# Address residues of matmul operands in a hybrid attention layer: unpadded key rows, small tiles in a pool of their own, padded projection weights

## The chip, the cores and the metric

The kernel runs on one core of one Trainium2 chip. A core has five engines that run beside each other: TensorE (PE in the profile, with its weight loads as PEld), VectorE (DVE), ScalarE (ACT), GpSimd (POOL) and SyncE (SP, which here issues most DMAs). The metric is the device time of one execution in microseconds (us), as the median of several runs. The profile is of one execution, with a span of its own.

A matmul takes two operands from the on-chip memory SBUF: a stationary one (128 columns here, brought in by a weight load of its own) and a moving one (up to 512 columns that stream past). The product is summed in PSUM. SBUF is 128 partitions, and a tile occupies the same byte range in each. "Residue" below means the byte at which an operand begins in its partition, modulo 512.

## The reference

One encoder layer on 2048 tokens of width 1024, all in float32. A combined projection feeds two groups of heads.

```python
h = x @ w_in                        # 1024 -> 2528 columns, split into the parts below
# group A: gated linear attention, 4 heads, key width 64, value width 128, chunks,
#          a forward and a backward scan, summed, RMSNorm per head, SiLU gate
o_a = gla_branch(g_q, g_k, g_v, g_gate, ...)
# group B: latent attention, 4 heads; dense softmax over all 2048 keys
q = (rms_norm(c_q) @ w_uq);  kv = (rms_norm(c_kv) @ w_ukv)
s = q_nope @ k_nope.T + q_rope @ k_rope.T
o_b = softmax(s) @ v * silu(gate)
x = layer_norm(alpha * x + concat(o_a, o_b) @ w_out)
```

## The kernel before, in words

**Split products.** Each float32 operand is held as two tiles of type float32r: a high part, rounded by a copy on ScalarE (`hi`, L366), and the rest, a subtraction on VectorE or GpSimd (`lo`, L373). A product is then three matmuls into one PSUM tile: high by high, low by high, high by low. `mm3` (L421, matmuls on L423, L424 and L425) writes them; the scores and two products of sweep C write theirs out by hand.

**Four stages**, in the order of time:

- *Sweep A* (`sweep_a`, L622), 16 chunks of 128 tokens from the last to the first. `products` (L755) multiplies a chunk (stationary: `xah`, `xal`, 8 row blocks k of 128) by the weights `wah` and `wal` (moving), in three column groups of 288, 384 and 384 columns (`A_GROUPS`, L27). The result is `ipa`. For most chunks 24 matmuls of 512 columns for the gate follow (`gate_products`, L842: result `ipg`, moving `wgh`/`wgl`). Between these stand the small products of the linear attention (L902 to L1043) and transposes by the identity.
- *Sweep C* (`sweep_c`, L1111), chunks in pairs from the first to the last: `pz` (L1221, 256 columns), `ipm` (L1292, 448 columns), norms, rotary tables. It leaves, for each of 16 key tiles of 128 keys, the compressed keys `ckvT_h`, `ckvT_l` (L1358, L1361), the rotary keys `kr` (tile name `krs`, L1364) and the values `vh`, `vl` in SBUF for the rest of the kernel. `vh` and `vl` have rows of 128 elements; the three key tiles have rows of `KW` = 132 elements, of which 128 are used (L549 to L551).
- *Attention* (`attention`, L1518), 16 blocks (4 heads by 4 blocks of 512 queries), each over 8 pairs of key tiles. For a pair, `scores` (L1544) writes 2 x 5 matmuls of 512 columns (L1552 to L1556): stationary a key tile, moving a query tile. Then ScalarE copies the scores out (L1561), VectorE keeps a running maximum (L1574), subtracts the maximum (L1598), ScalarE takes the exponential (L1602) and the high part `ph` (L1604), GpSimd the low part `pl` (L1609), and `pv` (L1632) writes 2 x 3 matmuls of 512 columns: stationary `vh`/`vl`, moving `ph`/`pl`. Per block there are three groups of four transposes by the identity (`mx` L1580, `mb` L1592, `sx` L1661) and three matmuls of 512 columns for `y` (L1698). So a block has 80 + 48 + 3 = 131 matmuls of 512 columns and 12 transposes.
- *Output projection* (`OutProj`): 16 chunks; moving `woh`/`wol`, stationary `oh`/`ol`, results `po`, `pmb`, `px` of 512 columns (the last chunk in part 256), residual, LayerNorm, store.

**Order.** The order on each engine is fixed by hand: tables of places (`PLACE`, `PLACE_LAST`, `PLACE_C` and the like) say at which step an operation of a pair is put, and `in_order` (L385) chains what comes out. The edits below change no entry of these tables.

**Places in SBUF.** Pools are laid one after another. Before the change most tiles begin at residue 448 (queries, values, chunks, gate weights, scores `s`). Others do not:

| operand (role) | residue before | residue after |
|---|---|---|
| queries `qh`, `ql`, `rh`, `rl` (moving, scores) | 448 | 448 |
| `ckvT_h`, `krs` of key tile kt (stationary, scores) | 192 + 16 kt | 448 |
| `ckvT_l` of key tile kt (stationary, scores) | 448 + 16 kt | 448 |
| `vh`, `vl` (stationary, pv) | 448 | 448 |
| `ph`, `pl` (moving, pv); `ofh` (moving, y) | 0 | 448 |
| `wah`, `wal`, row block k (moving, ipa) | 448 + 128 k, and 128 more for columns 288 on | 448 |
| `xah`, `xal` (stationary, ipa, ipg); `wgh`, `wgl` (moving, ipg) | 448 | 448 |
| `woh`, `wol` (moving, output projection) | 192 for k < 4, 448 for k >= 4 | 448 |
| `xch`, `xcl` (moving, pz) and `wzh`, `wzl` (stationary, pz) | 192 and 448 | the same |
| identity (moving, transposes) | 128 | 128 |

Row kt of a key tile lies 132 x 4 = 528 = 512 + 16 bytes after the row before it. A row block of `wah` is 1056 x 4 = 4224 = 8 x 512 + 128 bytes long, and its groups begin at columns 0, 288 and 672 (288 x 4 = 2 x 512 + 128; 672 x 4 = 5 x 512 + 128). `ph`, `pl` and `ofh` stand in pool `bp` (L1526) behind two tiles `mc` of 16 bytes, which take 32 bytes each.

Of the kernel before, what the change touches and what calls it, by code (L numbers as in the profile page):

```python
# [18 lines left out]
P = 128  # L19
S = 2048  # L20
D = 1024
NK = D // P
NCH = S // P
H = 4
NA = 1056
W_PIECES = ((2, 2, 2, 2), (2, 2, 2, 2), (2, 2, 2, 1, 1))
A_GROUPS = ((0, 288), (288, 384), (672, 384))  # L27
QB = 512
NQB = S // QB
NKT = S // P  # L30
KW = P + 4
TAU_INV = 1.0 / 16.0
RMS_EPS = 1e-6
LN_EPS = 1e-5
# [324 lines left out]
class K:  # L359
# [145 lines left out]
    def run(self):  # L505
        tc, nc, ins = self.tc, self.nc, self.ins
        with ExitStack() as top:
            cp = top.enter_context(tc.tile_pool(name="const", bufs=1))
            self.cp = cp
            dp = top.enter_context(tc.tile_pool(name="scr", bufs=1, space=DRAM))  # L510
            self.qd_s = [dp.tile([P, H * P], F32, name=f"qd_s{c}") for c in range(NCH)]
            self.oi_s = [dp.tile([P, H * P], F32, name=f"oi_s{c}") for c in range(NCH)]
            self.su_s = [dp.tile([P, H * P], F32, name=f"su_s{c}") for c in range(NCH)]
            self.u_s = [dp.tile([P, H * P], F32, name=f"u_s{c}") for c in range(NCH)]
            self.qa_s = [[dp.tile([P, H, QB], F32, name=f"q{p}_s{b}") for p in "hl"] for b in range(NQB)]
            self.qr_s = [[dp.tile([H, 64, QB], F32, name=f"r{p}_s{b}") for p in "hl"] for b in range(NQB)]
            self.gm_s = [dp.tile([P, H, QB], F32, name=f"gm_s{b}") for b in range(NQB)]
            self.oa_s = [dp.tile([P, H, P], F32, name=f"oa_s{c}") for c in range(NCH)]
            self.r_s = [dp.tile([1, H, QB], F32, name=f"r_s{b}") for b in range(NQB)]
            self.ob_s = [dp.tile([P, H, QB], F32, name=f"ob_s{b}") for b in range(NQB)]  # L520

            ident = cp.tile([P, P], F32, name="ident")
            self.ident = ident
            self.gkv_c = cp.tile([P, 1], F32, name="gkv_c")
            self.gn_c = cp.tile([P, 1], F32, name="gn_c")
            self.cw = cp.tile([P, NCH, 3, H], F32, name="cw")

            psum = ExitStack()
            pspool = lambda n: psum.enter_context(tc.tile_pool(name=n, bufs=2, space=PSUM, reuse_waits="tile"))
            self.gp, self.ip, self.tr = pspool("gp"), pspool("ip"), pspool("tr")  # L530
            self.xfp = top.enter_context(tc.tile_pool(name="xfp", bufs=2, reuse_waits="tile"))
            edge = top.enter_context(tc.tile_pool(name="edge", bufs=1, side="right"))
            edge.tile([P, 8], F32, name="edge")
            self.keep = top.enter_context(tc.tile_pool(name="keep", bufs=1, side="right", reuse_waits="tile"))
            wgs = ExitStack()
            self.wgp = wgs.enter_context(tc.tile_pool(name="wgp", bufs=2 * NK + 1, side="right", reuse_waits="tile"))
            self.xab = wgs.enter_context(tc.tile_pool(name="xab", bufs=2, side="right"))
            self.wgate = []
            self.wl = None
            self.sweep_a()  # L540
            self.wz = top.enter_context(tc.tile_pool(name="wz", bufs=2 * NK + 1, reuse_waits="tile"))
            bcs = ExitStack()
            self.wm = bcs.enter_context(tc.tile_pool(name="wm", bufs=2 * NK + 1, reuse_waits="tile"))
            self.bc = bcs.enter_context(tc.tile_pool(name="bc", bufs=1, reuse_waits="tile"))
            self.wl = bcs.enter_context(tc.tile_pool(name="wl", bufs=2, reuse_waits="tile"))
            self.late_gates()
            wgs.close()
            rp = top.enter_context(tc.tile_pool(name="res", bufs=1, side="right", reuse_waits="tile"))
            self.ckvT_h = rp.tile([P, NKT, KW], F32R, name="ckvT_h")  # L549
            self.ckvT_l = rp.tile([P, NKT, KW], F32R, name="ckvT_l")  # L550
            self.kr = rp.tile([P, NKT, KW], F32R, name="krs")  # L551
            self.vh = rp.tile([P, NKT, P], F32R, name="vh")
            self.vl = rp.tile([P, NKT, P], F32R, name="vl")
            self.sweep_c()
            bcs.close()
            psum.close()
            self.wof = top.enter_context(tc.tile_pool(name="wof", bufs=PRE_W, side="right", reuse_waits="tile"))
            self.attention()
# [63 lines left out]
    def sweep_a(self):  # L622
        tc, nc, ins, cp = self.tc, self.nc, self.ins, self.cp
        with ExitStack() as ctx:
# [1 line left out]
            xp, ip, tr, gp = self.xab, self.ip, self.tr, self.gp  # L626


            wah, wal = (wp.tile([P, NK, NA], F32R, name=f"wa{p}") for p in "hl")
            mask = wp.tile([P, P], I32, name="mask")  # L630
            rmask = wp.tile([P, H, P], F32, name="rmask")
            wg = wp.tile([98, H, P], F32R, name="wg")
# [17 lines left out]
            with tc.tile_pool(name="sta", bufs=1, reuse_waits="tile") as sta:  # L650
# [2 lines left out]
                wgf = sta.tile([98, H * P + 1], F32, name="wgf")  # L653
                wgh = sta.tile([98, H * P], F32R, name="wgh")
                wdone, worder = [], {}
                for g, (c0, n) in enumerate(A_GROUPS):
                    k = 0
                    for m in W_PIECES[g]:
                        if g == 0 and k in (0, NK // 2):
                            xs = slice(k, k + NK // 2)  # L660
                            nc.sync.dma_start(xf[:, xs], ins["xT"][NCH - 1][:, xs])
                            with self.in_order(worder):
                                self.hi(xcur[0][:, xs, 0], xf[:, xs])
                                self.lo(xcur[1][:, xs, 0], xf[:, xs], xcur[0][:, xs, 0])
                        st = sta.tile([P, m, n], F32, name=f"was{g}_{k}")
                        nc.sync.dma_start(st, ins[f"wA{g}"][:, k:k + m])
                        ks, cs = slice(k, k + m), slice(c0, c0 + n)
                        with self.in_order(worder):
                            for e in [slice(j, j + 1) for j in range(m)] if g == 0 else [slice(0, m)]:
                                kh, kl = wah[:, ks, cs][:, e], wal[:, ks, cs][:, e]  # L670
                                ops = self.hi(kh, st[:, e]), self.lo(kl, st[:, e], kh)
                        k += m
                        wdone.append(ops)
                    if g == 1:
                        nc.sync.dma_start(self.ident, ins["ident"])
# [79 lines left out]
    def products(self, d, g, after=lambda g, k: None):  # L755

        nc, c, i, g1 = self.nc, d["c"], d["i"], d["g1"]
        c0, n = A_GROUPS[g]
        xh, xl = d["x"]
        if i == 0 and g == 2:  # L760
            pt = self.gp.tile([P, 1024], F32, tag="gp", name=f"ipa{c}_{g}")
# [594 lines left out]
        self.lo(s["cqT_l"][:, :, j], d["tm"][:, 0:2], s["cqT_h"][:, :, j])  # L1356

    def c_ckvTh(self, d):  # L1358
        self.hi(self.ckvT_h[:, d["c"], :P], d["tm"][:, 2])

    def c_ckvTl(self, d):  # L1361
        self.lo(self.ckvT_l[:, d["c"], :P], d["tm"][:, 2], self.ckvT_h[:, d["c"], :P])

    def c_krT(self, d):  # L1364
        self.hi(self.kr[:, d["c"], :P], d["tm"][:, 3])


    def c_pqr(self, d):
# [149 lines left out]
    def attention(self):  # L1518
# [4 lines left out]
        with ExitStack() as ctx:  # L1523
            qp = self.wz
            sp = ctx.enter_context(tc.tile_pool(name="sp", bufs=NP + 4, reuse_waits="tile"))
            bp = ctx.enter_context(tc.tile_pool(name="bp", bufs=2, reuse_waits="tile"))  # L1526
            bank = lambda n, bufs=1: ctx.enter_context(tc.tile_pool(name=n, bufs=bufs, space=PSUM, reuse_waits="tile"))
            pM, pO, pX, pA, pS = bank("pM"), bank("pO"), bank("pX"), bank("pA"), bank("pS", 2)
            blocks = [(h, b) for b in range(NQB) for h in range(H)]
# [14 lines left out]
            def scores(i, j):  # L1544


                d = stt[i]
                qh, ql, rh, rl = d["q"]
                ps = d["ps", j] = pS.tile([P, 2, QB], F32, tag="pS", name=f"pS{i}_{j}")
                for e in range(2):  # L1550
                    kh, kl, kr = (t[:, 2 * j + e, :P] for t in (self.ckvT_h, self.ckvT_l, self.kr))
                    mm(ps[:, e], kh, qh, start=True, stop=False)  # L1552
                    mm(ps[:, e], kh, ql, start=False, stop=False)  # L1553
                    mm(ps[:, e], kl, qh, start=False, stop=False)  # L1554
                    mm(ps[:, e], kr, rh, start=False, stop=False)  # L1555
                    mm(ps[:, e], kr, rl, start=False, stop=True)  # L1556
# [24 lines left out]

            def rmax(i):
                d = stt[i]
                d["mc"] = bp.tile([P, 4], F32, tag="mc", name=f"mc{i}")
                V.tensor_reduce(d["mc"], d["x"], AX.X, ALU.max)

            def bmax(i):
# [75 lines left out]
            def rcp(i):  # L1663

                d = stt[i]
                rc = bp.tile([P, 4], F32, tag="rc", name=f"rc{i}")
                V.tensor_reduce(rc, d["x"], AX.X, ALU.add)
                V.reciprocal(rc, rc)
                d["rc"] = rc
# [11 lines left out]

            def rows(i):
                h, b = blocks[i]
                rr = bp.tile([4, P], F32, tag="rm", name=f"rt{i}", bufs=1)
                Ac.activation(rr, stt[i]["rt"], AF.Copy)
                nc.sync.dma_start(self.r_s[b][:, h].rearrange("o (e p) -> (o e) p", p=P), rr)

# [358 lines left out]
```

## Time and profile before

| | |
|---|---|
| median of 3 runs | 1305.8 us (1305.19 to 1305.91) |
| span of the profiled execution | 1302.9 us, 2.9 us less than the median |
| sweep A | to about 355 us |
| sweep C | about 355 to 609 us |
| attention | about 609 to 1113 us |
| output projection | about 1113 to 1303 us |
| TensorE busy | 1285.0 us of the span, 7082 matmuls |
| VectorE, ScalarE, GpSimd busy | 963.4, 816.7, 787.8 us |

How to read it: a span given for a matmul runs from its start to the modelled end of its drain, and the next matmul starts before that end. So the busy time of TensorE tells only that matmuls follow each other without a pause. How fast they follow is read from the distance of two starts, called pitch below. With matmuls of 512 columns that follow each other, the span is the pitch and a constant drain.

### The profile page before, as it was taken

How to read it: one execution, taken by the hardware profiler on the slowest of the kernel's cores; microseconds unless marked ns; L12 is line 12 of the kernel's file. 1: busy time of each engine (PE TensorE's matmuls, PEld its weight loads, DVE VectorE, ACT ScalarE, POOL GpSimd, SP SyncE). 2: the span in 40 equal slices, each digit the busy share in tenths (PEclk: the TensorE clock that was granted, in tenths of full speed). 3: DMA queues.
4: the chain of work that ended last, by engine and by line, in shares of the span. 5: the costliest groups of instructions: out<-in, count | busy, mean ns of one | idle time of the engine just before them, and what ended most of it. 6: DMA issues, size and time to landing. Idle time of an engine off the chain costs nothing.

```text
span 1302.9 us, 19959 instructions
## 1 busy us (share of the span) xinstructions
PE 1285.0 (99%) x7082; PEld 1130.4 (87%) x7082; DVE 963.4 (74%) x1706; ACT 816.7 (63%) x1334; POOL 787.8 (60%) x494
## 2 busy tenths in 40 slices
PE   8999999999999999999999999999999999999997
PEld 7999999999999999999788888888888888888886
DVE  7966665656674555554888888888888889469997
ACT  7765656565676566564778788878888888511110
POOL 0143233332467667661488888889999999944441
PEclk9999999999999999999999999999999999999999
DMA  8222213131566556656301111122123210366652
GB/s 293 66 89 61 87 53 94 51 95 49 171 232 194 187 178 205 206 173 213 87 1 41 41 42 41 41 60 63 58 70 99 51 41 9 122 204 205 215 192 98
DMA packets 105795, 145.81 MB, mean 112 GB/s; under 512 B 16630, under 2 KB 59262, under 8 KB 105696
## 3 DMA queue, kind: packets, MB, share of 16 engines
q1 hardware_dynamic: 97632, 142.41, 34.9%
q0 software_dynamic: 672, 2.10, 0.4%
q8 instruction: 56, 0.92, 0.3%
q10 hardware_dynamic: 7392, 0.03, 0.3%
q14 instruction: 43, 0.35, 0.1%
HBM read 94.14 MB, written 50.36 MB: 111 GB/s over the span
## 4 chain that ended last, share of the span: by engine, by line
PE 90%; POOL 2%; DVE 1%; ACT 1%; DMA 1%; issue 1%; DVEq 0%; POOLq 0%; SPq 0%
PE pz L1221 6%; PE ipm L1292 5%; PE o L423 5%; PE o L425 5%; PE o L424 5%; PE pS L1552 4%; PE pS L1555 4%; PE pS L1554 4%; PE pS L1556 4%; PE pS L1553 4%; PE ipa L423 4%; PE ipa L424 4%; PE ipa L425 4%; PE po L425 2%; PE po L423 2%; PE po L424 2%
## 5 line engine op out<-in xcount | busy, mean ns | idle before, releaser
L375 POOL TENSOR_TENSOR pl<-s,ph 128x1024 fp32r<-128x1024 f32 x128 | 306.8, 2411 | 65.8 <-ACT ph L369 60.6
L1574 DVE TENSOR_TENSOR rm<-pS,rm 128x512 f32<-128x512 f32 x210 | 144.8, 690 | 43.7 <-ACT s L1561 38.4
L1561 ACT ACTIVATE s<-pS 128x1024 f32<-128x1024 f32 x128 | 131.2, 1025 | 67.9 <-PE pS L1556 66.0
L1598 DVE TENSOR_TENSOR s<-s,mb 128x1024 f32<-128x1024 f32 x128 | 151.2, 1213 | 9.1 <-PE mb L1592 9.0
L1050 POOL TENSOR_TENSOR Us<-Us,cw 128x512 f32<-128x512 f32 x16 | 20.0, 1247 | 226.8 <-DVE Us L1048 188.3
L369 ACT ACTIVATE ph<-s 128x1024 fp32r<-128x1024 f32 x128 | 135.0, 1056 | 18.2 <-PE o L425 17.7
L1602 ACT ACTIVATE s<-s 128x1024 f32<-128x1024 f32 x128 | 131.4, 1050 | 12.3 <-DVE s L1598 12.2
L423 PE MATMUL ipa<-wah,xah 128*128 128x384 f32 (+1 forms) x384 | 129.6, 338 | 5.4 <-ACT wah L369 5.3
L424 PE MATMUL ipa<-wal,xah 128*128 128x384 f32 (+1 forms) x384 | 125.5, 327 | 0.0
L425 PE MATMUL ipa<-wah,xal 128*128 128x384 f32 (+1 forms) x384 | 124.9, 325 | 0.0
L1552 PE MATMUL pS<-qh,ckvT_h 128*128 128x512 f32 x256 | 103.8, 405 | 0.8 <-ACT s L1602 0.4
L423 PE MATMUL o<-ph,vh 128*128 128x512 f32 x256 | 102.6, 401 | 0.0
L425 PE MATMUL o<-ph,vl 128*128 128x512 f32 x256 | 101.3, 396 | 0.0
L1555 PE MATMUL pS<-rh,krs 128*128 128x512 f32 x256 | 101.2, 395 | 0.0
L424 PE MATMUL o<-pl,vh 128*128 128x512 f32 x256 | 101.1, 395 | 0.0
L1554 PE MATMUL pS<-qh,ckvT_l 128*128 128x512 f32 x256 | 100.9, 394 | 0.0
L1556 PE MATMUL pS<-rl,krs 128*128 128x512 f32 x256 | 100.7, 393 | 0.0
L1553 PE MATMUL pS<-ql,ckvT_h 128*128 128x512 f32 x256 | 100.6, 393 | 0.0
L1625 DVE TENSOR_TENSOR ap<-ap,s 128x512 f32<-128x512 f32 x120 | 83.1, 693 | 2.7 <-ACT s L1602 0.8
L375 POOL TENSOR_TENSOR ol<-of,oh 128x512 fp32r<-128x512 f32 x32 | 43.0, 1346 | 63.9 <-ACT oh L369 63.9
L423 PEld LDWEIGHTS ipa<-wah,xah 128*128 128x128 f32 x384 | 73.1, 190 | 6.2 <-ACT wah L369 5.3
L424 PEld LDWEIGHTS ipa<-wal,xah 128*128 128x128 f32 x384 | 73.2, 191 | 1.0 <-DVE wal L375 0.6
(325 smaller groups left out, 3841.2 us busy)
## 6 DMA issues: line engine op xcount, KB each, us to landing
xcf<-xT_dram SPq DMA_DIRECT2D x16, 512.0 KB, 5.5
xr<-x_dram SPq DMA_DIRECT2D x16, 512.0 KB, 6.5
out_dram<-rr SPq DMA_DIRECT2D x32, 256.0 KB, 2.2
xaf<-xT_dram SPq DMA_DIRECT2D x14, 512.0 KB, 4.2
oib<-oi_s SPq DMA_DIRECT2D x16, 256.0 KB, 4.6
qdb<-qd_s SPq DMA_DIRECT2D x16, 256.0 KB, 4.6
SU<-su_s SPq DMA_DIRECT2D x16, 256.0 KB, 5.0
ub<-u_s SPq DMA_DIRECT2D x16, 256.0 KB, 4.3
```

The source lines that it names most:

```text
L369: return nc.scalar.activation(dst, src, AF.Copy).ins
L375: return e.tensor_tensor(dst, src, hi.bitcast(F32), ALU.subtract).ins
L423: mm(out, ah, bh, start=start, stop=False)
L424: mm(out, ah, bl, start=False, stop=False)
L425: mm(out, al, bh, start=False, stop=stop)
L1552: mm(ps[:, e], kh, qh, start=True, stop=False)
L1553: mm(ps[:, e], kh, ql, start=False, stop=False)
L1554: mm(ps[:, e], kl, qh, start=False, stop=False)
L1555: mm(ps[:, e], kr, rh, start=False, stop=False)
L1556: mm(ps[:, e], kr, rl, start=False, stop=True)
L1574: V.tensor_tensor(d["rm"], src[:, e], d["rm"], ALU.max)
L1598: V.tensor_tensor(s, s, d["mb"][:, None, :].to_broadcast([P, 2, QB]), ALU.subtract)
```

## The change

Three edits; no instruction is added or taken away, and each engine keeps its order.

- Key rows have 128 elements in place of 132 (`KW` is gone), so each key tile kt begins a whole number of 512 bytes after the last.
- The small tiles of attention, `mc`, `rc` and the row tile of `rows`, go from pool `bp` to a new pool `bs` behind it, so the large tiles of `bp` move 64 bytes down.
- The weights of sweep A get rows of 1152 columns in place of 1056, and the three groups start at columns 0, 384 and 768 (`A_PLACE`) in place of 0, 288 and 672. The same columns are computed.

```diff
+NA_PAD = 1152
 A_GROUPS = ((0, 288), (288, 384), (672, 384))
+A_PLACE = (0, 384, 768)
-KW = P + 4
...
-            self.ckvT_h = rp.tile([P, NKT, KW], F32R, name="ckvT_h")
-            self.ckvT_l = rp.tile([P, NKT, KW], F32R, name="ckvT_l")
-            self.kr = rp.tile([P, NKT, KW], F32R, name="krs")
+            self.ckvT_h = rp.tile([P, NKT, P], F32R, name="ckvT_h")
+            self.ckvT_l = rp.tile([P, NKT, P], F32R, name="ckvT_l")
+            self.kr = rp.tile([P, NKT, P], F32R, name="krs")
...
-            wah, wal = (wp.tile([P, NK, NA], F32R, name=f"wa{p}") for p in "hl")
+            wah, wal = (wp.tile([P, NK, NA_PAD], F32R, name=f"wa{p}") for p in "hl")
...
-                        ks, cs = slice(k, k + m), slice(c0, c0 + n)
+                        ks, cs = slice(k, k + m), slice(A_PLACE[g], A_PLACE[g] + n)
...
-        c0, n = A_GROUPS[g]
+        c0, n = A_PLACE[g], A_GROUPS[g][1]
...
     def c_ckvTh(self, d):
-        self.hi(self.ckvT_h[:, d["c"], :P], d["tm"][:, 2])
+        self.hi(self.ckvT_h[:, d["c"]], d["tm"][:, 2])
...
+            bs = ctx.enter_context(tc.tile_pool(name="bs", bufs=2, reuse_waits="tile"))
...
-                d["mc"] = bp.tile([P, 4], F32, tag="mc", name=f"mc{i}")
+                d["mc"] = bs.tile([P, 4], F32, tag="mc", name=f"mc{i}")
...
-                rc = bp.tile([P, 4], F32, tag="rc", name=f"rc{i}")
+                rc = bs.tile([P, 4], F32, tag="rc", name=f"rc{i}")
...
-                rr = bp.tile([4, P], F32, tag="rm", name=f"rt{i}", bufs=1)
+                rr = bs.tile([4, P], F32, tag="rm", name=f"rt{i}", bufs=1)
```

Because the weights of sweep A are longer, what stands behind them in SBUF moves up by 6144 bytes, and tiles of sweep C come to lie on other tiles of sweep A than before. Some waits at the passage between the two sweeps are therefore on other instructions; the order is the same.

More of the change, by code (lines that the diff above doesn't have):

```diff
@@ L655, in sweep_a @@
                 wdone, worder = [], {}
-                for g, (c0, n) in enumerate(A_GROUPS):
+                for g, (_, n) in enumerate(A_GROUPS):
                     k = 0
@@ L1358, in c_ckvTh @@
     def c_ckvTh(self, d):
-        self.hi(self.ckvT_h[:, d["c"], :P], d["tm"][:, 2])
+        self.hi(self.ckvT_h[:, d["c"]], d["tm"][:, 2])
     def c_ckvTl(self, d):
-        self.lo(self.ckvT_l[:, d["c"], :P], d["tm"][:, 2], self.ckvT_h[:, d["c"], :P])
+        self.lo(self.ckvT_l[:, d["c"]], d["tm"][:, 2], self.ckvT_h[:, d["c"]])
     def c_krT(self, d):
-        self.hi(self.kr[:, d["c"], :P], d["tm"][:, 3])
+        self.hi(self.kr[:, d["c"]], d["tm"][:, 3])
     def c_pqr(self, d):
@@ L1550, in scores @@
                 for e in range(2):
-                    kh, kl, kr = (t[:, 2 * j + e, :P] for t in (self.ckvT_h, self.ckvT_l, self.kr))
+                    kh, kl, kr = (t[:, 2 * j + e] for t in (self.ckvT_h, self.ckvT_l, self.kr))
                     mm(ps[:, e], kh, qh, start=True, stop=False)
```

## Prediction

> **What bounds the kernel now.** I read the page first, then busy time by stage.
>
> ```profile
> span 1302.9 us, 19959 instructions
> ...
> PEclk9999999999999999999999999999999999999999
> ```
>
> ```profile
> core 0: us, PE busy (x) PEld busy (x) DVE busy (x) ACT busy (x) POOL busy (x), PEclk, DMA share, GB/s
> 0.00:325.00 325.00, 318.40 (x2004) 302.79 (x2005) 220.44 (x388) 201.63 (x389) 95.93 (x70) 1.00 0.31 94
> 325.00:720.00 395.00, 391.47 (x2481) 357.15 (x2480) 253.99 (x627) 258.99 (x526) 248.40 (x210) 1.00 0.49 156
> ```
>
> ```profile
> 627.90:655.60 27.70, 25.89 (x114) 20.16 (x113) 23.95 (x32) 22.19 (x24) 16.30 (x7) 1.00 0.11 29
> ...
> 719.10:1068.20 349.10, 349.10 (x1574) 283.94 (x1573) 296.97 (x397) 283.93 (x306) 307.12 (x134) 1.00 0.20 54
> ...
> 1200.00:1290.00 90.00, 90.00 (x402) 74.53 (x401) 87.34 (x130) 13.15 (x36) 38.18 (x30) 1.00 0.55 184
> ```
>
> TensorE never pauses from 719.1 to 1068.2 us, eleven blocks of attention (31.74 us each), at a full granted clock. VectorE, ScalarE and GpSimd have 52, 65 and 42 us left there. Only the first two blocks hold pauses (25.89 of 27.70 us in the second). So the time is the sum of the matmuls' pitches, and the question is what pitch the change gives. The change removes no instruction.
>
> The pitch is read from starts on the timeline. First the output projection:
>
> ```profile
> 1230.04 0.39 PE L423 MATMUL pmb<-woh,oh 128*128 128x512 f32 x1
> ...
> 1232.76 0.39 PE L423 MATMUL pmb<-woh,oh 128*128 128x512 f32 x1
> ```
>
> Twelve starts in 2.72 us: 226.7 ns for 512 columns. Then attention, scores and pv:
>
> ```profile
> 830.72 0.39 PE L1553 MATMUL pS<-ql,ckvT_h 128*128 128x512 f32 x1
> ...
> 832.58 0.39 PE L1556 MATMUL pS<-rl,krs 128*128 128x512 f32 x1
> ...
> 836.52 0.40 PE L423 MATMUL o<-ph,vh 128*128 128x512 f32 x1
> ...
> 837.92 0.40 PE L423 MATMUL o<-ph,vh 128*128 128x512 f32 x1
> ```
>
> Eight scores in 1.86 us, 232.5 ns; six pv in 1.40 us, 233.3 ns. The same instruction with the same 512 columns is 6 ns slower in attention. In the output projection both operands lie at the same residue modulo 256 (192 or 448 against 448); in pv they differ by 64, in the scores by 16 kt. Is it the place or the busy neighbours? Sweep C answers: `pz` has its operands at 192 and 448, equal modulo 256, while the other engines are busy some 65% (second row above). The chain of waits there:
>
> ```profile
> 415.65 2.87 PE pz L1221 x24
> ```
>
> 2.87 / 24 = 119.6 ns for 256 columns. Both pitches are the columns at one rate plus one constant: (226.7 - 119.6) / 256 = 0.418 ns a column, which leaves 12.5 ns. So neighbours do not lift the constant to the 18.5 ns or more that attention shows. I take the residue as the cause.
>
> **The change part by part.** *Attention.* For the sum I use mean spans, since span less pitch is constant: 389 - 226.7 = 162.3 in the output projection, 395 - 232.5 = 162.5 in the scores. The groups of 719.1 to 1068.2 us, then of 1200 to 1290 us:
>
> ```profile
> L1552 PE MATMUL pS<-qh,ckvT_h 128*128 128x512 f32 x176 | 71.3, 405 | 0.0
> L423 PE MATMUL o<-ph,vh 128*128 128x512 f32 x176 | 70.6, 401 | 0.0
> L425 PE MATMUL o<-ph,vl 128*128 128x512 f32 x177 | 70.1, 396 | 0.0
> L424 PE MATMUL o<-pl,vh 128*128 128x512 f32 x176 | 69.6, 395 | 0.0
> L1555 PE MATMUL pS<-rh,krs 128*128 128x512 f32 x176 | 69.6, 395 | 0.0
> L1554 PE MATMUL pS<-qh,ckvT_l 128*128 128x512 f32 x176 | 69.4, 394 | 0.0
> L1556 PE MATMUL pS<-rl,krs 128*128 128x512 f32 x176 | 69.2, 393 | 0.0
> L1553 PE MATMUL pS<-ql,ckvT_h 128*128 128x512 f32 x176 | 69.2, 393 | 0.0
> ```
>
> ```profile
> L425 PE MATMUL po<-woh,ol 128*128 128x512 f32 x67 | 26.1, 389 | 0.0
> L423 PE MATMUL po<-woh,oh 128*128 128x512 f32 x66 | 25.7, 389 | 0.0
> L424 PE MATMUL po<-wol,oh 128*128 128x512 f32 x66 | 25.7, 389 | 0.0
> ```
>
> ```profile
> L1552 PE MATMUL pS<-qh,ckvT_h x176: 390/396/479, 719.1 to 1065.0; 128*128 128x512 f32 x176
> ```
>
> Scores, per key tile: 405 + 393 + 394 + 395 + 393 = 1980, less 5 x 389 = 35 ns. L1552 holds the first matmul after a group of transposes, two of 16 per block, 479 where the median is 396. That price stays, so 2 x 83 / 16 = 10.4 goes off: 24.6 ns. Pv: 401 + 396 + 395 - 3 x 389 = 25, less one such matmul of 16 (5.2): 19.8 ns. Sixteen key tiles: 16 x (24.6 + 19.8) = 710 ns a block, at most.
>
> Not all of it comes. A stream at equal residues needs some matmuls to settle after a strange one. `ipg` of sweep A (448 against 448), after the small product `Op`:
>
> ```profile
> 237.23 0.39 PE L424 MATMUL ipg<-wgl,xah 128*128 128x512 f32 x1
> ...
> 238.61 0.39 PE L424 MATMUL ipg<-wgl,xah 128*128 128x512 f32 x1
> ...
> 239.52 0.39 PE L425 MATMUL ipg<-wgh,xal 128*128 128x512 f32 x1
> ```
>
> Six pitches in 1.38 us, 230.0 ns, then four in 0.91 us, 227.5. So 6 x 3.3 + 4 x 0.8 = 23 ns per disturbance; up to 40 if it lasts longer. A block has three groups of transposes, whose identity stays at 128. I take 30 each, 90 ns a block: 0.62 us a block net. For the fourteen blocks from the third on, 8.7 us. In the first two, TensorE waits in part for others, and I count 0.2 each. Attention: 9.1 us.
>
> *Sweep A.* Half of the row blocks k lie at 64 or 320, 128 away from the chunk at 448. Two triples of 384 columns, the first at 320, the second at 448:
>
> ```profile
> 140.25 0.34 PE L423 MATMUL ipa<-wah,xah 128*128 128x384 f32 x1
> ...
> 140.78 0.34 PE L423 MATMUL ipa<-wah,xah 128*128 128x384 f32 x1
> ...
> 141.30 0.28 PE L1042 MATMUL Up<-VV,kth 128*128 128x256 f32 x1
> ```
>
> 0.53 against 0.52 us, 10 ns at this rounding (0 to 20). There are 4 such k x 2 groups x 16 chunks = 128 triples: 1.0 us (0 to 2.6). For 288 columns I take nothing.
>
> *Output projection.* `woh` moves from 192 to 448 for half of its k; both already run at 226.7 (the rows from 1230.04 to 1232.76 hold both kinds): 0.
>
> *What else moves.* `ph`, `pl` and `ofh` go from 0 to 448 for the engines that write and read them. GpSimd's own rows show tiles at both places:
>
> ```profile
> L375 POOL TENSOR_TENSOR pl<-s,ph 128x1024 fp32r<-128x1024 f32 x88 | 211.0, 2410 | 41.0 <-ACT ph L369 36.8 <-POOL pl L375 3.7
> L1630 POOL TENSOR_TENSOR acc<-acc,s 128x1024 f32<-128x1024 f32 x23 | 55.6, 2417 | 0.9
> ```
>
> `acc` and `s` lie at 448: 7 ns of 2410, so I take 0. The waits that move between the sweeps concern stores and loads near 355 to 366 us; I put -0.5 to +1 us there, and take 0. A faster TensorE needs its inputs 0.6 us earlier per 31.7 us; GpSimd, the fullest of the others, is busy 307.12 of 349.1 us, 27.9 us a block, and would still have 3 us.
>
> Sum: 9.1 + 1.0 = 10.1 us off 1302.9, 1292.8 us of span, and with the 2.9 us by which the median exceeds the span, **1295.7 us**.
>
> **The rivals.** *Only constant places count* (0.14). In the scores the stationary tile changes every one or two matmuls, and that may be what costs. Key tile 0 speaks for it: its rows are at 192 and 448 already, equal to the queries modulo 256, and still:
>
> ```profile
> 909.51 0.39 PE L1552 MATMUL pS<-qh,ckvT_h 128*128 128x512 f32 x1
> ...
> 910.66 0.40 PE L1552 MATMUL pS<-qh,ckvT_h 128*128 128x512 f32 x1
> ```
>
> 1.15 / 5 = 230 ns. Against it: those five come between pv at other residues and key tile 1, and the settling above lasts six to ten matmuls. If it holds, pv alone gains, 16 x 19.8 ns x 16 blocks = 5.1 us, plus 1.0, less 0.9 for settling: 1300.6 us.
>
> *Place does not matter* (0.08). Attention's 6 ns would then come from something that attention alone has, such as two engines that read PSUM beside the matmuls. Then 1305.8 us. Against it stand `pz` under load and pv's steady 233.3. The Trainium skill leans this way: "TensorE: Matmul & The Clock Gate", "Step-by-step: what each phase is for", gives weight loads a read port apart from the moving operand's, so that loading does not slow the running matmul. By it the sum of this change would be 0; the two pitches above agree poorly with it.
>
> *Meeting at one place* (0.04), the slower side. With all at 448, GpSimd's two reads and write walk through the same residues as TensorE's, and might meet. Decisive is GpSimd's 27.9 us a block: it becomes the bound past 31.7, when its 11 long passes (eight `pl`, three `acc`) grow by 3.8 / 11 = 0.35 us each, 14%. At 20%, 0.48 us, it ends 1.5 us later per block, 14 x 1.5 = 21 us: 1327 us. The 2417 against 2410 speaks against it.
>
> **How the numbers follow.** Forecast 0.72, with its own range 1292.6 to 1299: low with no settling, all 16 blocks at 0.71 (11.4) and sweep A at its end of 2.6, less 0.8 that the pausing blocks keep; high with 40 ns per disturbance, no gain in sweep A, 1 us lost at the passage, 0.9 lost to waits. The rivals have 0.14, 0.08 and 0.04; 0.02 is for the unknown. The range 1292.6 to 1301.5 takes in the first rival and leaves some 0.15 out. Measurement can tell 0.2%, 2.6 us, from no change: faster 0.86 (forecast and first rival), same 0.09, slower 0.05.
>
> **What would show it.** In the changed profile: steady blocks of 31.1 us in place of 31.74; mean spans of pS and o near 390 to 392, L1552 and L423 some 8 above by their disturbed ones; triples of `ipa` all at 0.52; `pl` at 2.41 us; the granted clock at 1.00; no new idle time before L1552 or L424 from the third block on. Scores that stay at 393 to 395 while pv falls to 389 make the first rival right, unchanged spans the second, a longer `pl` the third.

## The result, and the profile after

The changed kernel takes 1295.38 us (median of 4 runs, 1295.25 to 1296.66), the kernel before beside it 1305.49 us (4 runs, 1304.71 to 1305.91): a ratio of 0.9928, with a 95% interval of 0.9914 to 0.9942. The prediction was 1295.7.

The profiled execution took 1295.28 us, its span is 1293.4 us. Of the page of the changed kernel, the span and the granted clock:

```profile
span 1293.4 us, 19959 instructions
...
PEclk9999999999999999999999999999999999999999
```

The span is 9.5 us shorter at the same full clock, with the same number of instructions. In the table by stage (columns as in the prediction: PE busy first, then the other engines) the next row holds the same eleven blocks of attention as 719.10:1068.20 of the kernel before:

```profile
core 0: us, PE busy (x) PEld busy (x) DVE busy (x) ACT busy (x) POOL busy (x), PEclk, DMA share, GB/s
...
716.70:1058.90 342.20, 342.20 (x1575) 283.36 (x1574) 297.02 (x397) 283.98 (x306) 306.19 (x133) 1.00 0.21 55
```

TensorE still never pauses, over 342.2 us in place of 349.1: 31.11 us a block against 31.74. The other engines do the same work as before there (GpSimd 306.2 against 307.1 us), so in this stretch nothing but the matmuls' pitch has moved. The groups of TensorE in that stretch (busy us, then the mean span of one in ns):

```profile
L1554 PE MATMUL pS<-qh,ckvT_h 128*128 128x512 f32 x177 | 70.9, 400 | 0.0
L424 PE MATMUL o<-ph,vh 128*128 128x512 f32 x176 | 69.5, 395 | 0.0
L426 PE MATMUL o<-ph,vl 128*128 128x512 f32 x177 | 69.0, 390 | 0.0
L1557 PE MATMUL pS<-rh,krs 128*128 128x512 f32 x176 | 68.6, 390 | 0.0
L1556 PE MATMUL pS<-qh,ckvT_l 128*128 128x512 f32 x176 | 68.6, 390 | 0.0
L1558 PE MATMUL pS<-rl,krs 128*128 128x512 f32 x176 | 68.6, 390 | 0.0
L1555 PE MATMUL pS<-ql,ckvT_h 128*128 128x512 f32 x176 | 68.5, 389 | 0.0
L425 PE MATMUL o<-pl,vh 128*128 128x512 f32 x176 | 68.5, 389 | 0.0
```

All eight lines fell by 4 to 6 ns, six of them to 389 or 390, as in the output projection; L1554 and L424 keep the dearer matmuls behind the transposes. On the timeline of the changed kernel, two starts with 30 matmuls between them:

```profile
830.70 0.39 PE L1554 MATMUL pS<-qh,ckvT_h 128*128 128x512 f32 x1
...
837.73 0.39 PE L1558 MATMUL pS<-rl,krs 128*128 128x512 f32 x1
```

That is 31 pitches in 7.03 us, 226.8 ns, in scores and pv alike.

Where the 9.5 us came from, as the start of the same matmul in both traces (after less before):

| place | difference, us |
|---|---|
| end of sweep A (last `ipg`, at 367.9 us of the kernel before) | -0.6 |
| second `ipm` of sweep C | -0.2 |
| first score, block 0 | -0.08 |
| first score, block 1 | -0.73 |
| first score, block 2 | -1.07 |
| first score, block 15 | -9.34 |
| pv at 1111.7 us of the kernel before, ahead of the output projection | -10.0 |
| last pv of attention, at 1151.4 us of the kernel before | -10.5 |
| `pmb` of chunk 6 (output projection) | -10.5 |
| `y` of the last block | -9.5 |
| end | -9.5 |

Thirteen blocks give 8.27 us, 0.636 each. The pv of the last block stand between the first products of the output projection, so attention gains until its last pv; 1.0 us is lost again after that. The rows ahead of attention say little about the change: the nine kernels traced here that have the padded weights reach the last `ipg` from 1.15 us earlier (d256) to 1.03 us later (d32) than the kernel before, with the same instructions up to there. The waits of TensorE in the changed kernel (engine, line and tile, what released it, us, times) name the places; the four rows below have no like among the kernel before's waits of 0.3 us and more, and the `rt` waits have none there at all:

```profile
engine line waited for: us in total, times, longest us
...
PE ipa L425 <- DVE wal L376: 0.5, 1, 0.5
PE rt L1681 <- ACT rt L1687: 0.5, 1, 0.5
PE Ob L1451 <- POOL qlb L376: 0.4, 1, 0.4
...
PE rt L1681 <- DVE rc L1669: 0.2, 1, 0.2
```

One stands at the start of the program (`ipa`, which reaches the low half of its weights before VectorE has made it), one at the start of sweep C (`Ob`), two in the output projection (`rt`, the row sums of the last block of attention). The `rt` waits do not come from TensorE being early. Eight of the nine kernels with padded weights have 0.2 to 0.9 us of them, e3_weights among them, which is only 0.6 us early there, and d128 and d192, which are 1.1 us late. Of the four with the old weights only e2_small has one, of 0.2 us; e12, 10.2 us early, has none. So they go with the padded weights more than with the pace of attention, and why is open.

### The profile page after: what moved, and what is told of

Its sections match the earlier page's. It is cut to its first block, busy times and chain, and to the rows that moved or that the text cites. A ratio compares the mean times of both kernels' runs of the same rounds, so it can differ in the third digit from the quotient of the medians.

```text
span 1293.4 us, 19959 instructions
## 1 busy us (share of the span) xinstructions
PE 1273.7 (98%) x7082; PEld 1127.9 (87%) x7082; DVE 962.8 (74%) x1706; ACT 816.2 (63%) x1334; POOL 786.1 (61%) x494
## 4 chain that ended last, share of the span: by engine, by line
PE 85%; DVE 4%; issue 2%; POOL 2%; ACT 1%; DMA 1%; SPq 0%; DVEq 0%; POOLq 0%
PE pz L1222 6%; PE ipm L1293 5%; PE o L424 4%; PE o L425 4%; PE o L426 4%; PE pS L1554 4%; PE pS L1556 4%; PE pS L1557 4%; PE pS L1555 4%; PE pS L1558 4%; PE ipa L424 4%; PE ipa L426 4%; PE ipa L425 4%; PE ipg L424 2%; PE ipg L425 2%
## 5 line engine op out<-in xcount | busy, mean ns | idle before, releaser
L424 PE MATMUL ipa<-wah,xah 128*128 128x384 f32 (+1 forms) x384 | 129.0, 336 | 5.4 <-ACT wah L370 5.4
L1554 PE MATMUL pS<-qh,ckvT_h 128*128 128x512 f32 x256 | 102.6, 401 | 0.8 <-DVE rm L1576 0.4
L424 PE MATMUL o<-ph,vh 128*128 128x512 f32 x256 | 101.0, 395 | 0.0
L424 PEld LDWEIGHTS ipa<-wah,xah 128*128 128x128 f32 x384 | 72.8, 190 | 6.6 <-ACT wah L370 5.6
```

The lines of the kernel that those rows point to most:

```text
L424: mm(out, ah, bh, start=start, stop=False)
```

## The experiments

Eleven kernels were run. Two of the theories come from the prediction: operands must agree modulo 256 (its forecast), or the change of the stationary tile is what costs, so that a constant place is enough (its first rival, as the expectations word it). The others come from what the first four runs left open. In the fences of this section stands, for each kernel, the row of the first matmul of each key tile: all 256 of them, with the shortest, the median and the longest span, and the start of the first and of the last. The distance of these two starts measures attention from its first score to the last key tile of block 15. For the kernel before it is 487.8 us:

```profile
L1552 PE MATMUL pS<-qh,ckvT_h x256: 387/396/496, 608.9 to 1096.7; 128*128 128x512 f32 x128
```

and for the changed kernel 478.0 us:

```profile
L1554 PE MATMUL pS<-qh,ckvT_h x256: 389/389/481, 608.8 to 1086.8; 128*128 128x512 f32 x128
```

| run | what it is | median, us | ratio to the kernel before (95%) | first to last start, us |
|---|---|---|---|---|
| e1_keys | key rows alone | 1301.09 | 0.9961 (0.9947 to 0.9976) | 484.0 |
| e2_small | small tiles alone | 1301.41 | 0.9962 (0.9947 to 0.9977) | 484.3 |
| e3_weights | weights alone | 1305.55 | 0.9996 (0.9986 to 1.0005) | 487.5 |
| e12 | key rows and small tiles | 1295.45 | 0.9930 (0.9915 to 0.9945) | 478.2 |
| d32 | all of it, keys and values 32 off | 1307.02 | 1.0010 (1.0001 to 1.0020) | 489.1 |
| d64 | the same, 64 off | 1299.32 | 0.9946 (0.9930 to 0.9963) | 481.9 |
| d128 | the same, 128 off | 1307.04 | 1.0011 (1.0002 to 1.0021) | 488.8 |
| d192 | the same, 192 off | 1307.52 | 1.0019 (1.0009 to 1.0029) | 489.3 |
| d256 | the same, 256 off | 1296.08 | 0.9926 (0.9911 to 0.9940) | 477.9 |
| pv0 | all of it, both operands of pv at 0 | 1299.39 | 0.9957 (0.9942 to 0.9971) | 482.0 |
| e8_ident | all of it, identity at 448 | 1295.21 | 0.9920 (0.9905 to 0.9935) | 478.4 |

**The parts alone.** Key rows alone (e1_keys):

```diff
-            self.ckvT_h = rp.tile([P, NKT, KW], F32R, name="ckvT_h")
-            self.ckvT_l = rp.tile([P, NKT, KW], F32R, name="ckvT_l")
-            self.kr = rp.tile([P, NKT, KW], F32R, name="krs")
+            self.ckvT_h = rp.tile([P, NKT, P], F32R, name="ckvT_h")
+            self.ckvT_l = rp.tile([P, NKT, P], F32R, name="ckvT_l")
+            self.kr = rp.tile([P, NKT, P], F32R, name="krs")
...
```

Expected:

> The kernel before with the key rows at 128 elements and nothing else. In the scores both operands then lie at 448; pv keeps 0 against 448, the weights of sweep A keep their four residues. Theory 'equal residues' (a matmul of 512 columns that follows others of its kind takes 226.7 ns where its two operands are equal modulo 256, more elsewhere): mean spans of the scores fall from 393-395 to 389-391, pv stays at 395-396; but pv and scores now alternate every 6 and 10 matmuls, and after each change some matmuls settle (about 20 ns), so of 0.39 us a block 0.2 to 0.39 is left: blocks of 31.35 to 31.55 us, 1300 to 1303 us in all. Rival 'place does not matter': 31.74, 1305.5.

Measured: 1301.09 us, 4.7 off the 1305.75 us of the kernel before in these runs. Its row, and two starts each from a run of scores that follows scores, and one that follows pv:

```profile
L1552 PE MATMUL pS<-qh,ckvT_h x256: 389/393/496, 608.6 to 1092.6; 128*128 128x512 f32 x128
```

```profile
861.06 0.39 PE L1552 MATMUL pS<-qh,ckvT_h 128*128 128x512 f32 x1
...
862.19 0.40 PE L423 MATMUL o<-ph,vh 128*128 128x512 f32 x1
...
863.58 0.40 PE L1552 MATMUL pS<-qh,ckvT_h 128*128 128x512 f32 x1
...
865.90 0.40 PE L423 MATMUL o<-ph,vh 128*128 128x512 f32 x1
```

Five scores up to the pv at 862.19 take 1.13 us, 226.0 ns each: the pitch is there. The ten scores from 863.58 take 2.32 us, 232.0 each, though each of them has equal operands: they follow six pv whose operands still differ by 64, and they are through before they settle. Two groups of pv, which this run does not touch, got faster too, against the expectation that pv would stay (mean spans; in the kernel before 396 and 395; the third group, with the matmuls behind the transposes, went from 401 to 399):

```profile
L425 PE MATMUL o<-ph,vl 128*128 128x512 f32 x182 | 71.6, 393 | 0.0
L424 PE MATMUL o<-pl,vh 128*128 128x512 f32 x182 | 71.2, 391 | 0.0
```

So a matmul's pitch depends on its neighbours and not on its own operands alone.

Small tiles alone (e2_small):

```diff
-                d["mc"] = bp.tile([P, 4], F32, tag="mc", name=f"mc{i}")
+                d["mc"] = bs.tile([P, 4], F32, tag="mc", name=f"mc{i}")
```

Expected:

> The kernel before with the small tiles in a pool of their own and nothing else: ph, pl and ofh move from 0 to 448 and are equal to vh, vl; the scores keep their changing key residues. 'Equal residues': pv falls from 395-396 towards 389-391, scores stay at 393-395; blocks of 31.42 to 31.6 us (16 x 19.8 ns less settling), 1301 to 1303.5 us. If the gains of this run, of the key rows alone and of the weights alone add up to less than the 10.1 us of all three, settling between unequal neighbours is worth the rest. 'Place does not matter': 1305.5.

```profile
L1553 PE MATMUL pS<-qh,ckvT_h x256: 387/394/481, 608.9 to 1093.2; 128*128 128x512 f32 x128
```

Measured: 1301.41 us, 4.3 off. Key tile 0 decides about the first rival: its residues are those of the kernel before (192 and 448), and its stationary tile changes as often as any. In the ninth block:

```profile
844.29 0.39 PE L1553 MATMUL pS<-qh,ckvT_h 128*128 128x512 f32 x1
...
845.42 0.39 PE L1553 MATMUL pS<-qh,ckvT_h 128*128 128x512 f32 x1
```

Five pitches take 1.13 us, where the prediction read 1.15 in the kernel before. Read to the nanosecond, they are 226 or 227 ns each in every block from the third on; in the eighth block of the kernel before they were 231, 235, 229, 232 and 229. These five follow pv that now agree too, and a stationary tile that changes, here between 192 and 448, costs them nothing.

Weights alone (e3_weights):

```diff
+NA_PAD = 1152
...
 A_GROUPS = ((0, 288), (288, 384), (672, 384))
+A_PLACE = (0, 384, 768)
...
-            wah, wal = (wp.tile([P, NK, NA], F32R, name=f"wa{p}") for p in "hl")
+            wah, wal = (wp.tile([P, NK, NA_PAD], F32R, name=f"wa{p}") for p in "hl")
...
```

Expected:

> The kernel before with the padded weights of sweep A and nothing else. From the profile of the changed kernel: sweep A ends 0.6 us earlier, 0.5 us of that is lost again before attention (a matmul of Ob waits 0.36 us longer for GpSimd); attention unchanged at 31.74 us a block. 1305.2 to 1305.6 us, not to be told from the kernel before by its time; the profile tells: the start of pz0 0.6 us earlier, of the first scores 0.1 us earlier.

Measured: 1305.55 us, a ratio whose interval holds 1. Against the kernel before the trace is 0.6 us early at the end of sweep A, 0.3 at the second `ipm` and at the first score, 0.6 at block 15, and 0.1 late at the end. The waits named above, `Ob` and `rt`, are in this run as well, 0.4 and 0.5 us. In the first 60 us TensorE pauses 6.66 us in place of 6.25, but that cannot be put down to the weights: the nine traces with padded weights have 6.0 to 8.0 us of pauses there, the four with the old ones 5.9 to 6.25.

Key rows and small tiles without the weights (e12). Expected:

> The kernel before with key rows unpadded and the small tiles moved, and the weights of the first sweep as before: both parts of attention without the third part. Theory L (the parts of attention add up to all of the gain there and more than their single gains, since with both no change of the residue is left inside a block; the weights give 0.6 us at the end of the sweep of which 0.3 is left at attention): a block of 31.10 us, first score 0.1 to 0.3 us later than in the changed kernel, 1295.5 to 1296.0 us. Theory M (single gains add up: 4.66 + 4.34): a block of 31.26 us, 1296.7 us. Had the weights been worth the 1.0 us of the prediction, 1296.4 us.

```profile
L1553 PE MATMUL pS<-qh,ckvT_h x256: 389/389/478, 608.9 to 1087.1; 128*128 128x512 f32 x128
```

Measured: 1295.45 us, span 1292.7, a block of 31.13 us. Theory L holds and M falls, by the blocks: from 31.74 us they lose 0.24 with the key rows alone, 0.23 with the small tiles alone, and 0.61 with both. The medians, 10.3 us off together and 4.7 + 4.3 = 9.0 alone, point the same way, but each has an interval of some 2 us on either side. The first score is 0.04 us later than in the changed kernel, not 0.1 to 0.3. This run has no `rt` wait and ends as early as the changed kernel does: of the weights nothing that can be measured is left at the end.

**How far apart may they be?** The changed kernel with pads ahead of the key and value tiles and behind them; here 64, the others alike:

```diff
+            rp.tile([P, 112], F32, name="pad0")
             self.ckvT_h = rp.tile([P, NKT, P], F32R, name="ckvT_h")
...
             self.vl = rp.tile([P, NKT, P], F32R, name="vl")
+            rp.tile([P, 16], F32, name="pad1")
```

Expected of 64 (d64):

> The changed kernel with 448 bytes of padding ahead of the key and value tiles and 64 behind: these stationary tiles all lie at 384, the moving ones at 448, in scores and pv alike; constant, but 64 apart. y, sweep A and the output projection as in the changed kernel. 'Equal residues': every score and pv at 233.3 ns (mean span 395-396), blocks of 31.75 to 31.85 us, 1305 to 1306 us. Rival 'only constant places count' (it costs when the stationary residue changes from tile to tile): 226.7 ns, blocks of 31.1 us, 1295.4 us.

```profile
L1556 PE MATMUL pS<-qh,ckvT_h x256: 388/392/482, 608.8 to 1090.7; 128*128 128x512 f32 x128
```

```profile
860.09 0.39 PE L1556 MATMUL pS<-qh,ckvT_h 128*128 128x512 f32 x1
...
865.82 0.39 PE L425 MATMUL o<-pl,vh 128*128 128x512 f32 x1
```

Measured: 1299.32 us. Twenty-five pitches in 5.73 us, 229.2 ns, in scores and pv alike. Both theories missed: a constant difference is not free, and it does not cost the 6.6 ns that pv paid in the kernel before with the same 64. The pitches run in a cycle of three, 226, 229 and 232 ns. Hence the next four. Two of their expectations give the pads wrongly: the edit puts 384 bytes ahead of the tiles and 128 behind for d128, 480 and 32 for d32. The residues and differences that they name are those of the kernels.

Expected of 256, 128, 32 and 192:

> The changed kernel with 256 bytes of padding ahead of the key and value tiles and 256 behind them: in attention every key tile and value tile lies at residue 192 modulo 512, every moving tile at 448, so the two operands differ by a constant 256. Theory A (the two operands must agree modulo 256, as in the output projection of the kernel before): a matmul every 226.7 ns, a block of 31.10 us, 1295.4 us (1295.0 to 1296.7). Theory B (they must agree modulo 512, or lie at the one place 448; 256 is then a constant difference like the 64 that was tried): 229.1 ns or more, a block of 31.37 us or more, 1299.3 us or more.

> The changed kernel with 128 bytes of padding ahead of the key and value tiles and 384 behind: the operands of scores and of probabilities times values differ by a constant 128. Theory C (any constant difference that is not a multiple of 256 costs the same 2.4 ns of a matmul as the 64 did, and the rest of what the kernel before lost came from changes of the difference between matmuls): 229.1 ns, a block of 31.37 us, 1299.3 us. Theory D (the cost grows with the difference up to 128): 231.5 ns, a block of 31.65 us, 1303.2 us. Theory E (a constant difference costs nothing by itself, 64 is special): 226.7 ns, 1295.4 us.

> The changed kernel with 96 bytes of padding ahead of the key and value tiles and 416 bytes in all in the other direction, so that they lie at residue 416 and the moving tiles at 448: a constant difference of 32. Theory C (every difference costs alike): 229.1 ns, 1299.3 us. Theory D (the cost grows with the difference): 227.9 ns, a block of 31.24 us, 1297.3 us.

> The changed kernel with the key and value tiles at residue 256 and the moving tiles at 448: a constant difference of 192, which is 64 less than 256. Theory H (the loss depends on the distance to the next multiple of 256, on either side): as with 64, 229.1 ns, a block of 31.37 us, 1299.3 us. Theory I (the sign decides too): another pitch, up to the 233.3 ns of 32, a block of up to 31.85 us, 1307 us.

The rows of d256, d128, d32 and d192, in this order:

```profile
L1556 PE MATMUL pS<-qh,ckvT_h x256: 389/389/481, 607.8 to 1085.7; 128*128 128x512 f32 x128
```

```profile
L1556 PE MATMUL pS<-qh,ckvT_h x256: 390/393/482, 609.1 to 1097.9; 128*128 128x512 f32 x128
```

```profile
L1556 PE MATMUL pS<-qh,ckvT_h x256: 393/396/481, 610.0 to 1099.1; 128*128 128x512 f32 x128
```

```profile
L1556 PE MATMUL pS<-qh,ckvT_h x256: 393/394/483, 608.5 to 1097.8; 128*128 128x512 f32 x128
```

And two starts of d192:

```profile
862.87 0.39 PE L1558 MATMUL pS<-qh,ckvT_l 128*128 128x512 f32 x1
...
865.90 0.39 PE L426 MATMUL o<-ph,vl 128*128 128x512 f32 x1
```

With 256 between the operands every span is that of the changed kernel: theory A holds against B, and agreement modulo 512 or one common place is not needed. With 32, 128 or 192 the kernel is slower than before by 1.6 to 1.8 us, little more than its scatter; d192 shows 13 pitches in 3.03 us, 233.1 ns, without a break, and a block of d32 takes 31.85 us against 31.74. So a constant relation is not enough (64 keeps 6.4 of the 10.1 us, the other three none): the first rival falls here too. So do theories C, D, E and H: the cost does not grow with the difference (64 is the cheapest of those that cost), and 192 is not like 64. Theory I is left, with no rule behind it.

**Whose operands must agree?** In pv0 the value tiles and `ph`, `pl` move together to 0:

```diff
+            rp.tile([P, 16], F32, name="pad0")
             self.vh = rp.tile([P, NKT, P], F32R, name="vh")
             self.vl = rp.tile([P, NKT, P], F32R, name="vl")
+            rp.tile([P, 112], F32, name="pad1")
...
+            bp.tile([P, 8], F32, tag="pad", name="pad2")
```

Expected:

> The changed kernel with the operands of probabilities times values (value tiles and the tiles of the split weights) moved together from residue 448 to 0, while those of the scores stay at 448. Each matmul's own two operands still agree; what differs by 64 is the stationary operand of one group against the moving operand of the other, where the groups meet (some fourteen times in a block). Theory J (a matmul's own pair must agree): 226.7 ns, a block of 31.10 to 31.15 us, 1295.4 us. Theory K (what one matmul streams must agree with what is loaded beside it for the next, or the place itself must stay): each meeting is followed by some ten matmuls of settling as in the run with the key rows alone, a block of about 31.5 us, 1301 us.

```profile
L1557 PE MATMUL pS<-qh,ckvT_h x256: 389/391/497, 608.2 to 1090.2; 128*128 128x512 f32 x128
```

```profile
862.19 0.39 PE L1557 MATMUL pS<-qh,ckvT_h 128*128 128x512 f32 x1
...
863.35 0.39 PE L1557 MATMUL pS<-qh,ckvT_h 128*128 128x512 f32 x1
...
864.48 0.39 PE L424 MATMUL o<-ph,vh 128*128 128x512 f32 x1
...
865.63 0.39 PE L426 MATMUL o<-ph,vl 128*128 128x512 f32 x1
```

Measured: 1299.39 us, a block of 31.37. Five scores behind pv take 1.16 us (232 ns each), the next five 1.13 (226), then five pv 1.15 (230). Every matmul has a pair that agrees, and a change between scores and pv still costs three to ten matmuls of settling; pv that run on long enough reach 226 and 227 ns at residue 0 as well. Theory J falls. Theory K has the mechanism and too high a price: it expected some 31.5 us a block and 1301 us, as in e1_keys. A block loses 0.26 us against the changed kernel where e1_keys lost 0.40. The wording of theory J, a matmul's own pair, is too weak: neighbours in the stream must agree as well. Whether it is the stationary tile loaded beside a running matmul that must agree with what streams, or the place of one moving tile with the next, this run does not tell.

**The transposes' identity** (e8_ident):

```diff
+            cp.tile([P, 80], F32, name="pad0")
             ident = cp.tile([P, P], F32, name="ident")
+            cp.tile([P, 48], F32, name="pad1")
```

Expected:

> The changed kernel with the identity of the transposes moved from residue 128 to 448 (pads in its pool). Theory F (a change of the difference between the operands costs some ten matmuls of settling, and the transposes between scores and probabilities times values are such a change): up to 90 ns of each of 16 blocks, 1293.9 to 1295.2 us. Theory G (transposes disturb nothing that the trace shows: the first matmuls behind them run at 226 to 228 already): 1295.4 us, within 0.1%.

```profile
L1556 PE MATMUL pS<-qh,ckvT_h x256: 389/389/497, 608.5 to 1086.9; 128*128 128x512 f32 x128
```

Measured: 1295.21 us, 0.2 us from the changed kernel and within the spread of either; the time lies at the edge of both theories and cannot tell. The trace does: the matmuls behind the transposes still settle, six or seven of them (four or ten in the changed kernel), so theory F falls. G is right about the time and not about its reason, since those matmuls do settle; what unsettles them is then not the identity's place.

No run beat the changed kernel by what can be measured.

## Why the prediction was right, and where it was not

*Attention, 9.1 us off.* Measured 10.4, from -0.08 at the first score to -10.5 at the last pv. Its price per matmul is right (226.7 ns predicted and found), and so is a steady block: 0.62 us predicted, 0.636 found. The settling term, 90 ns a block, comes out at 710 - 636 = 74. The term that was mis-sized is that of the two first blocks, 0.2 us each: sixteen blocks at 0.636 are 10.2 us, nearly all that was found. Pauses there did not swallow the gain, because TensorE waits only at a few places and runs at the new pitch between them.

*Its reason, operands equal modulo 256.* Shown by d256 against d32, d64, d128 and d192, with two corrections. The step that read pv's 233.3 ns as the price of its difference of 64 failed: d64 has the same 64 at 229.2, and two of pv's three groups in e1_keys, unchanged, got 3 to 4 ns cheaper. And agreement within each matmul is not enough, as pv0 shows. This fits the blocks of the parts, which lose 0.24 and 0.23 us alone and 0.61 together: alone, each leaves changes between the groups that keep the other from settling. Free were differences of 0 and 256; 32, 64, 128 and 192 were not, and no other difference was held constant over attention.

*Sweep A, 1.0 us off.* Both of its terms were mis-sized. From the start of the third chunk to the last `ipg`, behind the scatter of the start, the four kernels with the old weights take 332.73 to 332.78 us and the nine with the padded ones 332.26 to 332.52: some 0.35 us off. The gain is in the 288-column matmuls, which the prediction took as nothing: added up from start to next start, they fall there from 45.98 us to 45.58, and by the same 0.4 in every kernel with padded weights. The 384-column ones, from which it took the 1.0 us, go from 120.44 to 120.31 us, and stay between 120.3 and 120.5 whatever the weights. Three starts of the kernel before, then of the changed kernel, which begin the second and the third triple behind a small product, and the one that follows:

```profile
142.75 0.34 PE L423 MATMUL ipa<-wah,xah 128*128 128x384 f32 x1
...
143.27 0.34 PE L423 MATMUL ipa<-wah,xah 128*128 128x384 f32 x1
...
143.80 0.34 PE L423 MATMUL ipa<-wah,xah 128*128 128x384 f32 x1
```

```profile
142.46 0.35 PE L424 MATMUL ipa<-wah,xah 128*128 128x384 f32 x1
...
143.00 0.33 PE L424 MATMUL ipa<-wah,xah 128*128 128x384 f32 x1
...
143.52 0.33 PE L424 MATMUL ipa<-wah,xah 128*128 128x384 f32 x1
```

The third triple falls from 0.53 us to 0.52, as predicted, and the second rises from 0.52 to 0.54. On average past the first 60 us the third (26 of them) falls from 530 ns to 520, and the second (37) rises from 524.5 to 533.9. This fits settling: the step that failed is that the prediction counted it in attention and not in sweep A, where short runs of triples follow a disturbance. What is gained there need not last either: the changed kernel loses 0.4 of its 0.6 us in the wait for GpSimd at `Ob`, and d256, which has no such wait, carries all of its 1.1 us to the first score. With e12 as the test, the weights are worth 0 at the end.

*Output projection and waits, 0.* The output projection kept its pitch but gave 1.0 us back between chunk 6 and the last `y`, 0.7 of it in the two `rt` waits; the forecast's range had 0.9 for such waits, its sum had none. These misses, +1.3 in attention, -0.9 in sweep A and -1.0 here, cancel to within 0.6 us of span (predicted 1292.8, found 1293.4). The median came out nearer than the span: in each run it is some 2.0 us above the span, and the prediction's 2.9 held 0.9 by which the execution profiled before lay under its median. That the sum is so close is luck, not accuracy.

*The rivals.* "Only constant places count" expected pv alone to gain; in the result the scores gained as well, and e2_small's key tile 0 and d32, d128 and d192 refute it too. "Place does not matter" is refuted by the result. By the rule of the Trainium skill that the prediction named beside it ("TensorE: Matmul & The Clock Gate", "Step-by-step: what each phase is for") the change would have been worth 0; the trace disagrees by 9.5 us. "Meeting at one place" predicted longer passes of GpSimd; in the same eleven blocks of the changed kernel:

```profile
L376 POOL TENSOR_TENSOR pl<-s,ph 128x1024 fp32r<-128x1024 f32 x88 | 210.4, 2407 | 35.1 <-ACT ph L370 31.9 <-POOL pl L376 3.2
```

2407 ns against 2410: GpSimd does not mind.

*Open.* Why 64 is cheaper than 32, 128 and 192; why the same 64 ran at two pitches; which two neighbours must agree; and why the padded weights bring the `rt` waits. No run here tells.

## What to carry to other kernels

Where TensorE is the bound and one large matmul follows the next, read the pitch from starts and compare it between stages: a stage that pays more for the same shape is worth a look at the residues of its operands. Put the stationary and moving tiles of the whole stream at one residue modulo 256; partly aligned streams, or pairs that agree only among themselves, brought here about half of the gain (4.3 to 6.4 of 10.1 us), and a constant offset can cost as much as a mixture. Count what settles behind every disturbance: in the short runs of sweep A nearly all that the 384-column matmuls had to gain went there. A gain of a few tenths of a microsecond is not read from where one trace stands, when traces with the same instructions differ there by 2 us, but from a stretch without their scatter.

## What the runs showed of the hardware that was not expected

- The pitch of a 512-column matmul in this stream, with a weight load for each: 226.7 ns where stationary and moving operands agree modulo 256, 229.2 at 64 apart, and about 233 at 32, 128 and 192 apart, in fixed patterns (227, 227, 226; at 64: 226, 229, 232; at 192: 234, 233, 233).
- One relation can have two pitches: pv with its operands 64 apart ran at 233.3 ns in the kernel before, while scores and pv 64 apart ran at 229.2 in d64.
- After a change of place between neighbours (in pv0, where every pair of operands agrees), or a group of transposes, three to ten matmuls pass before the pitch is steady. In pv0 that costs 0.26 us of a block of 131 matmuls.
